# One order for all experts on three engines, outputs in two units of their own, and another depth of look-ahead

## The chip, the cores and the metric

The kernel runs on one core of one Trainium2 chip. The metric is the device time in microseconds (us) of one execution; three runs of the kernel before gave 1392.2, 1393.46 and 1393.85, so the median is 1393.46 us. Engines are named as in the profile: PE is TensorE (PEld its weight loads), DVE is VectorE, ACT is ScalarE, POOL is GpSimd, SP is SyncE, which here only issues transfers. A q after an engine's name is its sequencer.

## The reference

One decoder layer on 1024 tokens of width 1024. The first part (a gated MLP over chunks and differential attention, an output projection, cross-attention into 256 memory tokens) isn't touched by the change. The last part is a mixture of 32 experts with two experts for each token, and a norm:

```python
def hierarchical_moe(h, ...):            # t: 1024 tokens x 1024
    # group by softmax (top 1 of 4), then two of the 8 experts of that group, weights wts
    # tokens sorted by expert, in blocks of 128 rows, each block of one expert e
    def expert_rows(args):
        xb, e = args                      # xb: 128 x 1024
        g = xb @ w_gate[e]                # 1024 x 512
        u = xb @ w_up[e]                  # 1024 x 512
        return (jax.nn.silu(g) * u) @ w_down[e]   # 512 x 1024
    ...
    out = sum over the two experts of wts * y
x = x + hierarchical_moe(rms_norm(x, norm_ffn), ...)
return rms_norm(x, norm_final)
```

## The kernel before

All matmuls run in a form of float32 that is rounded, and each operand is split into a high part (a cast, on ACT) and a low part (the difference, on DVE). One product is then three matmuls (`mm3`, lines 135 to 138: high by high, high by low, low by high).

**An expert's work.** Expert e takes one block of up to 128 tokens. Its weights come as 12 tiles of 128 x 1024 (512 KB each): four of w_gate, four of w_up, four of w_down. Each tile is loaded by SP into a `raw` (line 271), split by ACT into `whi` (line 280) and by DVE into `wlo` (line 281), and used by six matmuls. `gather(e)` (line 1059) fetches the token rows by an indirect transfer of POOL into one of three `xg`. `x_t(e)` transposes them on PE (`px`, eight transposes, line 1414) and splits them into `xth` on ACT and `xtl` on DVE. `gate_up(e)` is 48 matmuls into two banks `pgu`, then Silu on ACT (`hh`, line 1436) and a product on DVE (`hh`, line 1437). `h_t(e)` turns `hh` (`pt`, four transposes, line 1444) and splits it into `ht`. `down(e)` is 24 matmuls into `py`, a copy `y` on ACT (line 1463) that applies the routing weight, and an indirect transfer of POOL that adds `y` to the rows of x2d in DRAM (line 1464), called the scatter here. A scatter waits until the one ahead of it has landed.

**The loop** (line 1489 on) does, for each e: `gate_up(e)`, `x_t(e + 1)`, `gather(e + 4)`, `down(e - 1)`, `h_t(e)`. After expert 1, `count_blocks` counts on PE and DVE how many blocks of 128 tokens are left over; at e = 4 that number is read into a register of each engine (line 1511), and a part behind the end, under `tc.If(nr > 0)`, handles leftover blocks. At e = 12 a row `gfin` for the last norm is loaded into a unit that stays taken.

**Memory.** `raw`, `whi`, `wlo`, `xth`, `xtl`, `ht`, `y`, `gfin` and the tiles of the end are *units*, 128 x 1024 words of float32 each, from one pool of NU = 45. A new tile takes a unit that is free in the program's order, and its writer waits for the last user of that unit. The planner `pump` issues loads up to `ahead["load"]` tiles ahead of the tile in use and splits up to `ahead["split"]` = 3 tiles ahead; each `take()` moves both on by one.

**Order.** SP and POOL always follow the order in which the program is written. PE, DVE and ACT follow it inside `tc.manual_schedule(engines=RM)`; outside, a scheduler places their instructions by a model of time. Before, the experts are outside from the end of expert 1 (`man.__exit__` at e = 1) to the start of the last pair (`last.__enter__` at e = 30). The look-ahead of the loads is `LF` = 10 from expert 16, ahead of that max(31, 30 - 2e) = 31.

Of the kernel before, what the change touches and what calls it, by code (L numbers as in the profile page):

```python
# [19 lines left out]
D = 1024  # L20
KT = 8
H = 512
NE = 32
NOV = 16
# [12 lines left out]
AL = 1  # L37
MD = 4.0
NX = 3
LA = 30  # L40
LE = 31
LD = 2
LS = 3
PF = 3
RM = {mybir.EngineType.DVE, mybir.EngineType.PE, mybir.EngineType.Activation}
PK = 12
LF = 10
EF = 16
JT = 0
ED = 1  # L50
KQ = lambda nc: nc.gpsimd
# [58 lines left out]
def tile_layer(tc, a, out):  # L110
    nc = tc.nc
# [11 lines left out]
    def unit(name, shape, dt=F32):  # L123
        return up.tile(shape, dt, name=name, tag="u", bufs=NU)
# [7 lines left out]
    def ps2(name="pd"):  # L132
        return psum.tile([128, 1024], F32, name=name, tag="pd", bufs=2)

    def mm3(o, sh, sl, mh, ml, start, stop):
        mm(o, sh, mh, start=start, stop=False)  # L136
        mm(o, sh, ml, start=False, stop=False)  # L137
        mm(o, sl, mh, start=False, stop=stop)  # L138
# [41 lines left out]
    def row(t, ap, n):  # L180
        nc.gpsimd.dma_start(t, bass.AP(tensor=ap.tensor, offset=ap.offset, ap=[[0, 128], [1, n]]))
# [81 lines left out]
    ahead = {"load": 3, "split": 1}  # L263
# [21 lines left out]
    def take():  # L285

        j = ptr["use"]
        ptr["use"] += 1
        pump()
        k = plan[j][1]  # L290
        return [t.rearrange("p (k c) -> p k c", k=k) for t in parts.pop(j)]
# [765 lines left out]
    def gather(e):  # L1057
        x = xg[e % NX]
        nc.gpsimd.indirect_dma_start(out=x, out_offset=None, in_=td[:, :],
                                     in_offset=bass.IndirectOffsetOnAxis(ap=idx[:, e:e + 1], axis=0),  # L1060
                                     bounds_check=S - 1, oob_is_err=False)
# [281 lines left out]
    man = tc.manual_schedule(engines=ORDS[0])  # L1343
# [39 lines left out]
    man = tc.manual_schedule(engines=ORDS[1])  # L1383
# [4 lines left out]
    man = tc.manual_schedule(engines=ORDS[2])  # L1388
# [6 lines left out]

    ahead["load"], ahead["split"] = LA, LS

    xts = {}
    def x_t(e):
        x = xg[e % NX]  # L1400
        if e == 0:
            xh, xl = unit("xth", [128, D], F32R), unit("xtl", [128, D], F32R)
            for i in range(2):
                p = ps1("px")
                cs = slice(512 * i, 512 * i + 512)
                for k in range(4):
                    nc.tensor.transpose(p[:, k * 128:(k + 1) * 128], x[:, (4 * i + k) * 128:(4 * i + k + 1) * 128],
                                        ident)
                split(xh[:, cs], xl[:, cs], p)
            xts[e] = (xh, xl)  # L1410
            return
        px = ps2("px")
        for k in range(KT):
            nc.tensor.transpose(px[:, k * 128:(k + 1) * 128], x[:, k * 128:(k + 1) * 128], ident)
        xh, xl = unit("xth", [128, D], F32R), unit("xtl", [128, D], F32R)
        split(xh, xl, px)
        xts[e] = (xh, xl)

    hts = {}

    def gate_up(e, between=None):
        xh, xl = xts.pop(e)
        gu = []
        for w in range(2):
            p = ps1("pgu")
            for q in range(4):
                wh, wl = take()
                for k2 in range(2):
                    k = 2 * q + k2
                    ks = slice(k * 128, (k + 1) * 128)  # L1430
                    mm3(p, xh[:, ks], xl[:, ks], wh[:, k2], wl[:, k2], k == 0, k == KT - 1)
            gu.append(p)
            if w == 0 and between:
                between()
        hh = half("hh")
        nc.scalar.activation(hh, gu[0], AF.Silu, scale=tab[:, 1, e:e + 1])
        nc.vector.scalar_tensor_tensor(hh, gu[1], tab[:, 1, e:e + 1], hh, op0=OP.mult, op1=OP.mult)
        hts[e] = hh

    def h_t(e):  # L1440
        hh = hts[e]
        pt = ps1("pt")
        for k in range(4):
            nc.tensor.transpose(pt[:, k * 128:(k + 1) * 128], hh[:, k * 128:(k + 1) * 128], ident)
        x = unit("ht", [128, 2, H], F32R)
        split(x[:, 0], x[:, 1], pt)
        hts[e] = x

    def down(e, between=None):
        x = hts.pop(e)  # L1450
        py = ps2("py")
        for k in range(4):
            wh, wl = take()
            ks = slice(k * 128, (k + 1) * 128)
            for c in range(2):
                cs = slice(c * 512, (c + 1) * 512)
                mm3(py[:, cs], x[:, 0, ks], x[:, 1, ks], wh[:, 0, cs], wl[:, 0, cs], k == 0, k == 3)
            if k == 1 and between:
                between()
        if e == NE - 1:  # L1460
            return py
        y = unit("y", [128, D])
        nc.scalar.activation(y, py, AF.Copy, scale=tab[:, 0, e:e + 1])  # L1463
        nc.gpsimd.indirect_dma_start(out=x2d[:, :], out_offset=bass.IndirectOffsetOnAxis(ap=idx[:, e:e + 1], axis=0),  # L1464
                                     in_=y, in_offset=None, bounds_check=S - 1, oob_is_err=False,
                                     compute_op=OP.add)

    man = tc.manual_schedule(engines=RM)
# [7 lines left out]
    novi = op.tile([128, 1], I32, name="novi")  # L1476

    def count_blocks():

        pc = ps1()  # L1480
        for t in range(8):
            mm(pc[:, :NE], oneb, Mb[t // 4][:, 3 + t % 4], start=(t == 0), stop=(t == 7))
        nc.vector.tensor_scalar(nb, pc[:, :NE], 128.0, None, op0=OP.is_gt)
        for j in range(2, 8):
            nc.vector.tensor_scalar(t1, pc[:, :NE], 128.0 * j, None, op0=OP.is_gt)
            nc.vector.tensor_add(nb, nb, t1)
        nc.vector.tensor_reduce(nov[:, 0:1], nb, axis=AX.X, op=OP.add)
        nc.vector.tensor_copy(novi, nov[:, 0:1])
    for e in range(NE):
        ahead["load"] = LF if e >= NE - EF else max(LE, LA - LD * e)  # L1490
        gate_up(e, between=(lambda: h_t(0)) if e == 1 else None)
        if e + 1 < NE:
            x_t(e + 1)
        if e + 1 + NX < NE:
            gather(e + 1 + NX)
        if e == NE - 2:
            last = tc.manual_schedule(engines=RM)
            last.__enter__()

            down(e - 1, between=lambda: h_t(NE - 2))  # L1500
            break
        if e:
            down(e - 1)
        if e:
            h_t(e)
        if e == 1:
            man.__exit__(None, None, None)
            count_blocks()
        if e == 4:
            with tc.manual_schedule(engines=RM):  # L1510
                nr = nc.values_load(novi[0:1, 0:1], min_val=0, max_val=NOV - 1,
                                    skip_runtime_bounds_check_because="2048 assignments leave at most 15 further blocks")
        if e == PK:
            gfin = unit("gfin", [128, D])
            row(gfin, a["norm_final"], D)


    e = NE - 1

    ahead["load"], ahead["split"] = 20, 5  # L1520
    down(e - 1)
    st = op.tile([128, 2, 9], F32, name="rfin")
    xf = [unit("xf", [128, D]) for _ in range(8)]
# [52 lines left out]
    for t in (0, 2, 3, 1, 4, 6, 5, 7):  # L1576
        store(t)
    nc.gpsimd.indirect_dma_start(out=out[:, :], out_offset=bass.IndirectOffsetOnAxis(ap=idx[:, NE - 1:NE], axis=0),  # L1578
                                 in_=sq[8], in_offset=None, bounds_check=S - 1, oob_is_err=False)
    last.__exit__(None, None, None)  # L1580

    ovu = {}
    ovp = [0]
# [15 lines left out]
    with tc.If(nr > 0):  # L1599
# [63 lines left out]
        with tc.For_i(0, nr, 1) as b:  # L1663
            eb = nc.values_load(eidd[bass.ds(b, 1), :], engines=[mybir.EngineType.SP], min_val=0, max_val=NE - 1,
                                skip_runtime_bounds_check_because="clamped to the last expert")
# [39 lines left out]
            y = unit("oy", [128, D])  # L1705
# [51 lines left out]
def _build(arrays):  # L1757
    import numpy as np
    import concourse.bacc as bacc
    nc = bacc.Bacc("TRN2", target_bir_lowering=False, num_devices=1)  # L1760
    a = {n[3:]: nc.dram_tensor(n, v.shape, mybir.dt.from_np(v.dtype), kind="ExternalInput").ap()
         for n, v in arrays.items()}
    out = nc.dram_tensor("out_0_dram", (S, D), mybir.dt.from_np(np.dtype("float32")), kind="ExternalOutput").ap()
    with tile.TileContext(nc, schedule_with_timeline_sim=True) as tc:
        tile_layer(tc, a, out)
    return nc
# [8 lines left out]
```

## Time and profile before

| | |
|---|---|
| median of three runs | 1393.46 us (1392.2 to 1393.85) |
| profiled execution | 1396.04 us, span of its instructions 1394.3 us |
| mean granted clock of TensorE | 0.974 |
| busy share of the span | PE 95%, PEld 82%, DVE 72%, ACT 60%, POOL 18% |
| moved by DMA | 322.39 MB, mean 231 GB/s |
| first matmul of an expert | 776.8 us |

The busy shares are means over the whole span. The experts fill the time from 776.8 us to about 1365 us, and there the engines are far busier than the means say; the part ahead of 776.8 us is the same program in both kernels.

### The profile page before, as it was taken

The page shows a single profiled execution, that of the slowest core. Times are in us where ns is not written, and L with a number is a line of the kernel's source. Part 1 is how long each engine was busy: PE and PEld are TensorE (multiplying, and loading weights), DVE is VectorE, ACT ScalarE, POOL GpSimd, SP SyncE. Part 2 cuts the span into 40 slices and gives each one's busy share as a digit, 9 for nine tenths or more (in the row PEclk, how much of TensorE's full clock was granted, in tenths as well). Part 3 has the DMA queues.
Part 4 walks back from the last instruction along what each step waited for, and adds up shares of the span by engine and source line. Part 5 has one row for each costly group of instructions (what it writes and reads, how often), then busy time and mean ns, then how long its engine had stood idle before and what let it go on. Part 6 is the DMA issues. An engine that isn't in the chain of part 4 may idle for free. (4 is left out here: it accounts for less than half of the span.)

```text
span 1394.3 us, 20530 instructions
## 1 busy us (share of the span) xinstructions
PE 1322.7 (95%) x7424; PEld 1146.8 (82%) x7424; DVE 1001.3 (72%) x1564; ACT 836.7 (60%) x1139; POOL 255.7 (18%) x284
## 2 busy tenths in 40 slices
PE   7999999999989999999998899999989999999981
PEld 6988998989888889998886687888778888888861
DVE  6776694767765543434365798999979999999984
ACT  6644553445455543333323587888868888888874
POOL 2521110411021321112112121111111111111110
PEclk9999999999999999999998799999999999999995
DMA  8720211320275664103799799999999699999986
GB/s 306 220 84 15 47 61 46 91 69 16 101 266 188 201 243 143 38 25 110 241 331 336 244 322 369 364 355 357 354 366 351 226 371 381 366 366 363 373 287 256
DMA packets 103226, 322.39 MB, mean 231 GB/s; under 512 B 15748, under 2 KB 23972, under 8 KB 103121
## 3 DMA queue, kind: packets, MB, share of 16 engines
q1 hardware_dynamic: 76896, 272.14, 53.4%
q0 software_dynamic: 17776, 40.51, 10.1%
q10 hardware_dynamic: 8448, 8.39, 1.8%
q8 instruction: 59, 0.97, 0.3%
q14 instruction: 47, 0.38, 0.1%
HBM read 287.10 MB, written 46.66 MB: 239 GB/s over the span
## 5 line engine op out<-in xcount | busy, mean ns | idle before, releaser
L281 DVE TENSOR_TENSOR wlo<-raw,whi 128x1024 fp32r<-128x1024 f32 (+1 forms) x469 | 559.6, 1231 | 75.3 <-ACT whi L280 62.6
L280 ACT CAST whi<-raw 128x1024 fp32r<-128x1024 f32 (+1 forms) x469 | 472.7, 1050 | 69.2 <-DVE wlo L281 11.9
L136 PE MATMUL pgu<-whi,xth 128*128 128x512 f32 x512 | 199.4, 398 | 4.3 <-ACT whi L280 3.2
L137 PE MATMUL pgu<-wlo,xth 128*128 128x512 f32 x512 | 201.2, 393 | 0.8 <-DVE wlo L281 0.8
L138 PE MATMUL pgu<-whi,xtl 128*128 128x512 f32 x512 | 201.0, 393 | 0.5 <-DVE xtl L142 0.5
L1464 POOL DMA_INDIRECT x2d<-y,idx x31 | 51.6, 1666 | 449.4 <-ACT y L1463 411.5
L136 PEld LDWEIGHTS pgu<-whi,xth 128*128 128x128 f32 x512 | 97.0, 190 | 26.0 <-ACT whi L280 5.2
L137 PEld LDWEIGHTS pgu<-wlo,xth 128*128 128x128 f32 x512 | 97.2, 190 | 22.3 <-DVE wlo L281 1.4
L138 PEld LDWEIGHTS pgu<-whi,xtl 128*128 128x128 f32 x512 | 97.0, 189 | 21.2 <-DVE xtl L142 1.2
L137 PE MATMUL py<-wlo,ht 128*128 128x512 f32 x256 | 103.7, 405 | 2.2 <-DVE wlo L281 2.2
L136 PE MATMUL py<-whi,ht 128*128 128x512 f32 x256 | 102.3, 399 | 1.5 <-ACT whi L280 0.8
L138 PE MATMUL py<-whi,ht 128*128 128x512 f32 x256 | 101.0, 394 | 0.0
L658 ACT ACTIVATE p<-p,stt 128x128 f32<-128x128 f32 (+7 forms) x64 | 49.6, 776 | 50.4 <-DVE stt L657 45.9
L136 PE MATMUL pp<-whi,hTh 128*128 128x256 f32 x256 | 74.6, 291 | 0.2 <-ACT whi L280 0.2
L137 PE MATMUL pp<-wlo,hTh 128*128 128x256 f32 x256 | 73.4, 287 | 1.3 <-DVE wlo L281 1.3
L136 PE MATMUL pp<-whi,h2h 128*128 128x256 f32 x256 | 73.1, 285 | 0.0
L138 PE MATMUL pp<-whi,hTl 128*128 128x256 f32 x256 | 73.1, 285 | 0.0
L137 PE MATMUL pp<-wlo,h2h 128*128 128x256 f32 x256 | 72.5, 283 | 0.0
L138 PE MATMUL pp<-whi,h2l 128*128 128x256 f32 x256 | 72.5, 283 | 0.0
L136 PE MATMUL pp<-hTh,whi 128*128 128x512 f32 x160 | 63.6, 397 | 0.4 <-ACT ot L710 0.4
L137 PE MATMUL pp<-hTl,whi 128*128 128x512 f32 x160 | 63.0, 394 | 0.0
L138 PE MATMUL pp<-hTh,wlo 128*128 128x512 f32 x160 | 62.8, 393 | 0.0
(365 smaller groups left out, 2942.4 us busy)
## 6 DMA issues: line engine op xcount, KB each, us to landing
raw<-in_w_gate SPq DMA_DIRECT2D x128, 512.0 KB
raw<-in_w_up SPq DMA_DIRECT2D x128, 512.0 KB
raw<-in_w_down SPq DMA_DIRECT2D x128, 512.0 KB
raw<-in_w_in SPq DMA_DIRECT2D x19, 512.0 KB
raw<-in_w_kv_mem SPq DMA_DIRECT2D x16, 512.0 KB
raw<-vwd SPq DMA_DIRECT2D x16, 512.0 KB
raw<-in_w_q_memT SPq DMA_DIRECT2D x8, 512.0 KB
raw<-in_w_out SPq DMA_DIRECT2D x8, 512.0 KB
```

Of the source, the lines that this page charges most:

```text
L136: mm(o, sh, mh, start=start, stop=False)
L137: mm(o, sh, ml, start=False, stop=False)
L138: mm(o, sl, mh, start=False, stop=stop)
L280: nc.scalar.copy(hi[:, c], raw[:, c])
L281: ahead.get("lo", nc.vector).tensor_tensor(lo[:, c], raw[:, c], hi[:, c].bitcast(F32), op=OP.subtract)
L658: nc.scalar.activation(pe[:, :nk], pe[:, :nk], AF.Exp, bias=stt[:, 2 + m:3 + m], scale=slopes[hd], accum_out=stt[:, 4 + m:5 + m])
L1464: nc.gpsimd.indirect_dma_start(out=x2d[:, :], out_offset=bass.IndirectOffsetOnAxis(ap=idx[:, e:e + 1], axis=0), in_=y, in_offset=None, bou ...
```

## The change

The experts are now one manual stretch on PE, DVE and ACT from expert 0 to the end of the kernel, so the three engines follow the order of the loop. The two tiles `ys` are taken once, ahead of the loop, and `y` of expert e is `ys[e % 2]`; the other tiles share 43 units. `ahead["load"]` is 29 up to expert 11 (e < PK = 12) and 27 from expert 12 on.

```diff
-LA = 30
-LE = 31
-LD = 2
+LA = 29
+LE = 29
 PK = 12
-LF = 10
-EF = 16
...
     hts = {}
+    ys = [unit("y", [128, D]) for _ in range(2)]
...
         if e == NE - 1:
             return py
-        y = unit("y", [128, D])
+
+        y = ys[e % 2]
         nc.scalar.activation(y, py, AF.Copy, scale=tab[:, 0, e:e + 1])
...
     for e in range(NE):
-        ahead["load"] = LF if e >= NE - EF else max(LE, LA - LD * e)
+        ahead["load"] = LE if e < PK else LE - 2
         gate_up(e, between=(lambda: h_t(0)) if e == 1 else None)
...
         if e == NE - 2:
-            last = tc.manual_schedule(engines=RM)
-            last.__enter__()
 
             down(e - 1, between=lambda: h_t(NE - 2))
             break
...
         if e == 1:
-            man.__exit__(None, None, None)
             count_blocks()
         if e == 4:
-            with tc.manual_schedule(engines=RM):
-                nr = nc.values_load(novi[0:1, 0:1], min_val=0, max_val=NOV - 1,
+            nr = nc.values_load(novi[0:1, 0:1], min_val=0, max_val=NOV - 1,
...
-    last.__exit__(None, None, None)
+    man.__exit__(None, None, None)
```

Line numbers of the changed kernel are two to five lower for the same statement.

**ACT in the steady part of the experts** (expert 20 and its neighbours). Before, one expert reads:

```order
L1463 ACTIVATE y<-py,tab 128x1024
L141 CAST ht<-pt 128x512
L280 CAST whi<-raw 128x1024 x4
L1436 ACTIVATE hh<-pgu,tab 128x512
L280 CAST whi<-raw 128x1024 x4
L141 CAST xth<-px 128x1024
L280 CAST whi<-raw 128x1024 x4
```

In the changed kernel the same stretch reads:

```order
L1462 ACTIVATE y<-py,tab 128x1024
L138 CAST ht<-pt 128x512
L277 CAST whi<-raw 128x1024 x8
L1434 ACTIVATE hh<-pgu,tab 128x512
L138 CAST xth<-px 128x1024
L277 CAST whi<-raw 128x1024 x4
```

The Silu moves four splits later, directly ahead of the split of the next expert's tokens. On PE the loop's order now holds word for word: all 48 matmuls of `gate_up(e)`, the eight transposes of `x_t(e + 1)`, the 24 matmuls of `down(e - 1)`, the four transposes of `h_t(e)`; before, both kinds of transposes stood between matmuls of `down`.

**ACT at the second tile of w_up of expert 13** (`whi_10020` before, `whi_9998` now), with the semaphores that each row waits for; DMAHW is a load by SP, DMASW an indirect transfer of POOL. Before:

```order
L280 CAST whi_9996<-raw_9572 128x1024 [waits DMAHW1_49,DVE_49]
L280 CAST whi_10008<-raw_9584 128x1024 [waits DMAHW2_49,PE_49]
L280 CAST whi_10020<-raw_9596 128x1024 [waits DMAHW3_49,DMASW0_49]
L280 CAST whi_10032<-raw_9608 128x1024 [waits DMAHW4_49,DMASW2_49,Activation_49]
L1436 ACTIVATE hh_10091<-pgu_9993,tab_96 128x512 [waits PE_49]
```

Now:

```order
L1462 ACTIVATE y_7662<-py_9908,tab_96 128x1024 [waits DMASW6_49,PE_49]
L138 CAST ht_9966<-pt_9961 128x512 [waits PE_49]
L277 CAST whi_9974<-raw_9581 128x1024 [waits DMAHW1_49]
L277 CAST whi_9986<-raw_9593 128x1024 [waits DMAHW2_49,DVE_49,PE_49]
L277 CAST whi_9998<-raw_9618 128x1024 [waits DMAHW3_49,DVE_49,PE_49]
L277 CAST whi_10010<-raw_9630 128x1024 [waits DMAHW4_49,DVE_49,PE_49]
```

Before, the unit of `whi_10020` was that of an earlier `y`, and the split waits until that `y`'s scatter has landed. Now no split up to expert 30 waits for a scatter; `y` itself waits for the scatter of two experts earlier.

**DVE after expert 1**, at `count_blocks` (`nb`, `t1`, `nov`: counts of 128 x 32). Before, from the split of the turned hidden tile on:

```order
L142 TENSOR_TENSOR ht_7984<-pt_7979,ht_7984 128x512
L1485 TENSOR_SCALAR t1_7686<-ps_7988 128x32
L1486 TENSOR_TENSOR nb_7685<-nb_7685,t1_7686 128x32
L281 TENSOR_TENSOR wlo_8016<-raw_7414,whi_8015 128x1024
L1485 TENSOR_SCALAR t1_7686<-ps_7988 128x32
L281 TENSOR_TENSOR wlo_8028<-raw_7416,whi_8027 128x1024
```

Now the whole count follows that split, and this is its end and what comes next:

```order
L1484 TENSOR_SCALAR t1_7688<-ps_7984 128x32
L1485 TENSOR_TENSOR nb_7687<-nb_7687,t1_7688 128x32
L1486 TENSOR_REDUCE nov_7689<-nb_7687 128x1
L1487 CAST novi_7690<-nov_7689 128x1
L278 TENSOR_TENSOR wlo_8012<-raw_7414,whi_8011 128x1024
```

The 15 small instructions of the count stood among the splits of expert 2; now all of them stand in one piece ahead of the next split. The read of the register stood in the last part of the program on PE, DVE and ACT, and now stands there at expert 5.

## Rows read from the trace of the kernel before

**Rows 1.** The page: busy us, share and instructions of each engine.

```profile
PE 1322.7 (95%) x7424; PEld 1146.8 (82%) x7424; DVE 1001.3 (72%) x1564; ACT 836.7 (60%) x1139; POOL 255.7 (18%) x284
```

**Rows 2.** Timeline of ACT: the Silu of experts 2, 4, 10, 12, 13, 16, 29.

```profile
818.69 0.69 ACT L1436 ACTIVATE hh<-pgu,tab 128x512 f32<-128x512 f32 x1 [0.33 <-PE pgu L138]
...
856.69 0.68 ACT L1436 ACTIVATE hh<-pgu,tab 128x512 f32<-128x512 f32 x1
...
963.07 0.68 ACT L1436 ACTIVATE hh<-pgu,tab 128x512 f32<-128x512 f32 x1
...
999.85 0.69 ACT L1436 ACTIVATE hh<-pgu,tab 128x512 f32<-128x512 f32 x1
...
1022.66 0.68 ACT L1436 ACTIVATE hh<-pgu,tab 128x512 f32<-128x512 f32 x1
...
1077.37 0.69 ACT L1436 ACTIVATE hh<-pgu,tab 128x512 f32<-128x512 f32 x1
...
1307.39 0.69 ACT L1436 ACTIVATE hh<-pgu,tab 128x512 f32<-128x512 f32 x1 [0.28 <-PE pgu L138]
```

**Rows 3.** Timeline of ACT: two splits, with the idle time ahead of them.

```profile
842.63 1.99 ACT L280 CAST whi<-raw 128x1024 fp32r<-128x1024 f32 x2 [3.23 <-DMA x2d<-y,idx]
...
1021.71 1.04 ACT L280 CAST whi<-raw 128x1024 fp32r<-128x1024 f32 x1 [4.30 <-issue]
```

**Rows 4.** Timeline of POOL: issues of four scatters.

```profile
832.31 1.59 POOL L1464 DMA_INDIRECT x2d<-y,idx  x1 [15.35 <-ACT y L1463]
...
1012.87 1.58 POOL L1464 DMA_INDIRECT x2d<-y,idx  x1 [14.58 <-DVE wlo L281]
...
1338.99 2.49 POOL L1464 DMA_INDIRECT x2d<-y,idx  x1 [16.48 <-ACT y L1463]
1350.42 2.41 POOL L1464 DMA_INDIRECT x2d<-y,idx  x1 [8.93 <-ACT whi L280]
```

**Rows 5.** Windows of 18 us: busy by engine, PEclk, DMA share, GB/s.

```profile
1005.00:1023.00 18.00, 15.03 (x70) 11.52 (x68) 12.33 (x13) 10.98 (x13) 3.30 (x3) 1.00 0.97 349
...
1077.00:1095.00 18.00, 18.00 (x87) 15.01 (x86) 16.60 (x16) 14.87 (x17) 3.02 (x2) 1.00 0.33 87
...
1329.00:1347.00 18.00, 17.22 (x76) 13.46 (x75) 16.30 (x16) 15.73 (x17) 2.49 (x1) 1.00 1.02 383
```

**Rows 6.** Waits of SP from 1060 to 1110 us: total, times, longest.

```profile
SPq L271 <- DVE wlo L281: 20.6, 4, 17.5
```

**Rows 7.** Timelines of PE and DVE in expert 1.

```profile
804.79 1.03 PE L1414 MATMUL px<-ident,xg 128*128 128x128 f32 x8
...
809.79 0.39 PE L136 MATMUL py<-whi,ht 128*128 128x512 f32 x1
...
806.91 1.23 DVE L142 TENSOR_TENSOR xtl<-px,xth 128x1024 fp32r<-128x1024 f32 x1 [0.31 <-ACT xth L141]
808.05 4.62 DVE L281 TENSOR_TENSOR wlo<-raw,whi 128x1024 fp32r<-128x1024 f32 x4
```

**Rows 8.** Timeline of DVE: the first and the fifth instruction of the count.

```profile
812.87 0.19 DVE L1483 TENSOR_SCALAR nb<-ps 128x32 f32<-128x32 f32 x1 [0.20 <-PE ps L1482]
...
813.65 0.22 DVE L1486 TENSOR_TENSOR nb<-nb,t 128x32 f32<-128x32 f32 x1
```

**Rows 9.** The tile novi: the register's read on PE's sequencer, ns and start.

```profile
L1511 PEldq TENSOR_LOAD <-novi x1: 491/491/491, 1361.1 to 1361.1; - x1
```

**Rows 10.** Waits of ACT from 1270 to 1360 us: total, times, longest.

```profile
ACT whi L280 <- DMA raw<-in_w_down: 8.8, 10, 1.8
```

**Rows 11.** Timelines of ACT, PE, SP at the end: outputs of experts 29, 30.

```profile
1337.59 1.12 ACT L1463 ACTIVATE y<-py,tab 128x1024 f32<-128x1024 f32 x1
...
1345.04 1.11 ACT L1463 ACTIVATE y<-py,tab 128x1024 f32<-128x1024 f32 x1
...
1357.17 0.66 PE L1444 MATMUL pt<-ident,hh 128*128 128x128 f32 x4 [2.90 <-DVE hh L1437]
...
1357.85 4.52 SPq L1526 DMA_DIRECT2D xf<-x2d  x8
```

More of the change, by code (lines that the diff above doesn't have):

```diff
@@ L1506, in tile_layer @@
         if e == 1:
-            man.__exit__(None, None, None)
             count_blocks()
         if e == 4:
-            with tc.manual_schedule(engines=RM):
-                nr = nc.values_load(novi[0:1, 0:1], min_val=0, max_val=NOV - 1,
-                                    skip_runtime_bounds_check_because="2048 assignments leave at most 15 further blocks")
+            nr = nc.values_load(novi[0:1, 0:1], min_val=0, max_val=NOV - 1,
+                                skip_runtime_bounds_check_because="2048 assignments leave at most 15 further blocks")
         if e == PK:
```

## The prediction

> **What bounds it now.** The page's busy shares [rows 1] put PE far ahead, but they are means over stages, so I read stage by stage. From 776.8 us on the experts run, and the Silu on ACT marks each expert once. From expert 16 to expert 29 it comes 13 times in 1307.39 - 1077.37 = 230.02 us, 17.69 us apart [rows 2], and the window there shows PE busy for all of its 18.00 us [rows 5]: in this stretch PE is the bound, and no order on the other engines can make it shorter. Elsewhere experts take longer. From 2 to 29 there are 488.70 us for 27 steps, where 27 x 17.69 = 477.63 would do: 11.07 us are lost. They sit in two places [rows 2]: 2 to 4 takes 38.00 us (2.62 too many), 10 to 16 takes 114.30 us (8.16 too many, of which 22.81 - 17.69 = 5.12 in the one step from 12 to 13); 4 to 10 loses 0.24, 16 to 29 loses 0.05.
>
> Next, why. In both bad steps one split on ACT stands idle for long: 3.23 us at 842.63, put down to the landing of a scatter, and 4.30 us at 1021.71 [rows 3]. The second has no releaser in the view, but the order of the kernel before shows that split waiting for an indirect transfer of POOL, and a scatter was issued at 1012.87 [rows 4], 8.84 us ahead; the first was issued at 832.31, 10.32 us ahead. A scatter lands about 9 to 10 us after its issue, and the unit of its `y` was given to a split.
>
> What is left of the second place (8.16 - 5.12 = 3.04 us) I put down to a shortage of units. With 31 raws, two `y`, four token tiles and one `ht` out of 45, about 7 units are left for whi and wlo, three and a half pairs, where the look-ahead of 3 wants four; `gfin` takes one more at expert 12. This cause is argued from a count, not read.
>
> Last the transfers. DMA is full nearly everywhere (share 0.97 and 1.02 in the first and last window of [rows 5]), except from 1077 to 1095 us, where it is 0.33: SP stands 17.5 us in one wait [rows 6], because the look-ahead falls from 31 to 10 at expert 16 and a load far ahead of its use has to wait for a unit. That loses 0.67 x 18 = 12.1 us of transfers, and nobody misses them until the end, where ACT waits ten times for loads, 8.8 us in all [rows 10]. So the loads are a second bound just behind PE.
>
> **The change, part by part.**
>
> *Stalls removed.* With `ys` apart, no split up to expert 30 waits for a scatter. The other tiles share 43 units: 43 - 29 raws - 4 - 1 leaves 9, from expert 12 on 43 - 27 - 1 - 4 - 1 = 10, more than four pairs. So both causes go, and I take all of it: -11.1 us. Bounds: at least the two steps with a landing (5.12 and most of 2.62, say -7), at most -11.1, since PE fills the rest. The new wait is that `y` waits for the scatter of two experts earlier; behind it on ACT stand `ht` and eight splits, and PE waits for these. It was issued 2 x 17.69 us earlier and lands within 10.3 us, so the cover is some 25 us; gone, it would cost the landing's 10 us per expert. A split near the end takes the unit of expert 29's output; its landing (by 1350.42 in the old trace, [rows 4]) comes ahead of PE's need for the last hidden tile.
>
> *The fixed order itself.* The trace holds a sample of it: expert 1 ran under the loop's order. PE starts the transposes at 804.79; DVE splits the tokens at 806.91 and then four weight tiles from 808.05, 4.62 us for four, so the first, which is the fourth tile of `down`, is done by 809.2; PE comes to that tile at 809.79 [rows 7]. The order keeps up with 0.6 us to spare, at the tightest place. Cost taken 0; bounds 0, and the rival below.
>
> On SP and POOL nothing changes place but the register's read, two rows earlier on SP, so every load, gather and scatter keeps its rank in its queue; only the units that they wait for differ.
>
> *The count on DVE in one piece.* Its first five instructions start 0.78 us apart over four steps [rows 8], 0.195 each, so 15 take 2.9 us, now ahead of the next split. DVE is busy 16.60 of 18 us [rows 5], so 1.4 us per expert can absorb it: +1.5 us once. Bounds 0 and 2.9.
>
> *The register.* It was read where PE had nothing urgent, 491 ns [rows 9]; now it stands between two experts on PE, DVE and ACT. On PE it can lie behind queued transposes (0) or in front of the matmuls (0.5). I take +0.5.
>
> *Look-ahead.* Starting with 29 instead of 31 makes the loads two tiles later where they are ahead, 2 x 17.69 / 12 = 2.9 us. The change from 29 to 27 at expert 12 holds back two loads for a moment, where 31 to 10 held back 21, so the 12.1 us come back. The stream of loads thus ends 12.1 - 2.9 = 9.2 us earlier. PE comes to the last experts 11.1 - 1.5 - 0.5 = 9.1 us earlier. The loads just follow: no gain and no loss at this point, but no slack either.
>
> *The end.* From `y` of expert 29 at 1337.59 to the first load of the sum at 1357.85 [rows 11] there are 20.26 us, made of two scatters in a row, 11.43 us from 1338.99 to 1350.42 and 7.43 us to 1357.85 [rows 4, 11]. `y` of expert 30 at 1345.04 is there in time and doesn't count; nor does PE's 2.90 us wait for the last `hh`, since what follows hangs on the loads of the sum. If the waits for loads shrink, `y` of expert 29 is up to 2.9 us less late (0 to 2.9, I take 1.0). The two scatters are 7.4 to 11.4 us each: -4.0 to +4.0 against now, taken 0 because transfers still run then. So -1.0 here.
>
> **The sum.** -11.1 + 1.5 + 0.5 - 1.0 = -10.1 us. The profiled execution took 1396.04 us (its span is 1394.3, with 1.7 around it), so it would take 1385.9. It is 2.6 us over the median of the runs, 1393.46, and the median goes to 1383.4 us, 0.7% less.
>
> One rule speaks against this. The window in which splits can run ahead gets narrower in the second half: with a look-ahead of 10 some 27 units were free for pairs, now 10. The rows say that this is enough, since experts 4 to 10 ran with about 7 and took 106.38 us for six, 17.73 each [rows 2]; by them the sum stays 1383.4. The Trainium skill (Perfetto Trace Analysis, Identifying Performance Opportunities) says that the same gap repeating on the engine that should be saturated can mean too little SBUF for the next tile; it gives no figure, and by it the third rival would hold, 1397.4.
>
> **Rivals.**
>
> *The loads are late* (0.18). The 9.2 us against 9.1 leave nothing, and the end already waits for loads [rows 10]. For it: DMA is full in every window but one. Against: the first half had loads long ahead. Every us that the stream lacks costs one; if it comes only half as early, 4.6 us are missing: 1388.0.
>
> *The end shortens* (0.12). If the loads are drained when expert 29's scatter goes, both scatters take the shorter time: -4.0 more, 1379.4.
>
> *A gap in every expert* (0.10), the other side. The 0.6 us at the fourth tile of `down` [rows 7] is thin, and expert 1 had loads and units in plenty. Should ACT come to a split late, the same gap returns 28 times. It decides from 10.1 / 28 = 0.36 us a time; at 0.5 us it costs 14: 1397.4.
>
> *The stalls stay* (0.08). If experts 10 to 16 lose their time to full transfers (0.97 at 1005 us, [rows 5]) and not to units, only the first place goes: -2.6 - 1.0 + 2.0 = -1.6, 1391.9.
>
> **Numbers.** The forecast has 0.52, and its own range is 1379 to 1387. With the late loads (0.18), and most of the short end (0.10 of 0.12), 0.80 lie from 1377.5 to 1391. About 0.2% (2.8 us) can be told from no change here. Faster: 0.52 + 0.12 + 0.16 of the late loads = 0.80. Same: the stalls that stay and the rest of the late loads, 0.10. Slower: 0.10.
>
> **What would show it.** In the changed profile the Silus should lie 17.7 us apart from expert 4 to 29, with some 2 us lost once near expert 2; no split waits for a landing; DMA has no window under 0.9 between 830 and 1320 us. Repeated idle time of PE with ACT or DVE as releaser would be the gap; waits of ACT for loads from expert 24 on would be the late loads. The prediction is wrong if DMA, once never idle, moves less in a time than it did, or if the fixed order makes PE wait at places that expert 1 does not show.

## The result, and the profile after

The changed kernel takes 1385.55 us (median; 1383.87 to 1386.86), the kernel before 1393.65 in the runs beside it (1392.2 to 1394.88). The ratio is 0.9938, 95% interval 0.9924 to 0.9952: 8.1 us faster, where 10.1 were forecast. A second measurement on another chip gave 1386.01 against 1392.36, ratio 0.9953 (0.9937 to 0.9969), 6.4 us. The profiled execution of the changed kernel took 1386.86 us, its span is 1385.2; that of the kernel before was 1396.04 and 1394.3, so in the traces 9.1 us are gone.

The page's busy row, which answers to [rows 1]: the counts of instructions are the same. PE's busy time falls by 4.6 us; part of that is stretches at the lower granted clock that the trace of before has and this one has not, shown under "The order alone" and "The sum".

```profile
PE 1318.1 (95%) x7424; PEld 1145.2 (83%) x7424; DVE 1001.0 (72%) x1564; ACT 842.3 (61%) x1139; POOL 245.7 (18%) x284
```

The Silus of [rows 2] are no good marks across the change, since their place among the splits on ACT has moved. The issue of an expert's scatter on POOL is one: it follows PE's last matmul of `down`. Timeline of POOL in the changed kernel, scatters of experts 1, 11, 14, 24, 28, 29 and 30 (start, us, line, what, and in brackets the idle time ahead of it):

```profile
831.68 1.59 POOL L1463 DMA_INDIRECT x2d<-y,idx  x1 [5.59 <-ACT y L1462]
...
1009.00 1.58 POOL L1463 DMA_INDIRECT x2d<-y,idx  x1 [5.61 <-ACT y L1462]
...
1062.39 1.58 POOL L1463 DMA_INDIRECT x2d<-y,idx  x1 [5.78 <-ACT y L1462]
...
1239.53 1.59 POOL L1463 DMA_INDIRECT x2d<-y,idx  x1 [5.60 <-ACT y L1462]
...
1313.04 1.80 POOL L1463 DMA_INDIRECT x2d<-y,idx  x1 [15.78 <-ACT y L1462]
1331.26 1.78 POOL L1463 DMA_INDIRECT x2d<-y,idx  x1 [16.43 <-ACT y L1462]
1341.87 1.56 POOL L1463 DMA_INDIRECT x2d<-y,idx  x1 [8.82 <-DMA x2d<-y,idx]
```

The same view of the kernel before for experts 14, 24 and 28; experts 1, 11, 29 and 30 stand in [rows 4].

```profile
1073.51 1.58 POOL L1464 DMA_INDIRECT x2d<-y,idx  x1 [14.45 <-ACT y L1463]
...
1249.97 1.59 POOL L1464 DMA_INDIRECT x2d<-y,idx  x1 [14.37 <-ACT y L1463]
...
1320.81 1.71 POOL L1464 DMA_INDIRECT x2d<-y,idx  x1 [15.76 <-ACT y L1463]
```

After less before: -0.6 us at expert 1, -3.9 at 11, -11.1 at 14, -10.4 at 24, then -7.8 at 28, -7.7 at 29, -8.5 at 30. So the two bad places are gone, and some 2.7 us are given back between experts 24 and 28. Windows of the changed kernel (busy by engine, PEclk, DMA share, GB/s):

```profile
1005.00:1023.00 18.00, 18.00 (x87) 14.96 (x86) 16.83 (x16) 15.15 (x18) 3.29 (x3) 1.00 0.98 368
1077.00:1095.00 18.00, 18.00 (x87) 14.96 (x86) 16.73 (x16) 15.39 (x17) 2.62 (x2) 1.00 0.98 356
1257.00:1275.00 18.00, 17.21 (x82) 13.96 (x82) 15.46 (x15) 14.15 (x17) 3.39 (x2) 1.00 1.03 378
1275.00:1293.00 18.00, 16.84 (x79) 13.64 (x78) 15.17 (x15) 14.26 (x16) 1.97 (x1) 1.00 0.97 358
1329.00:1347.00 18.00, 17.15 (x76) 13.88 (x74) 16.37 (x15) 15.18 (x16) 3.34 (x2) 1.00 0.83 272
```

Against [rows 5]: from 1005 us PE is now busy for all 18.00 us instead of 15.03, and the hole of the loads at 1077 (0.33) has closed (0.98). New are the two windows from 1257 us, where PE loses 0.79 and 1.16. Timeline of ACT there, the Silu of five experts and one split:

```profile
1231.15 0.67 ACT L1434 ACTIVATE hh<-pgu,tab 128x512 f32<-128x512 f32 x1
1249.99 0.68 ACT L1434 ACTIVATE hh<-pgu,tab 128x512 f32<-128x512 f32 x1
...
1266.69 1.05 ACT L277 CAST whi<-raw 128x1024 fp32r<-128x1024 f32 x1 [2.46 <-DMA raw<-in_w_down]
...
1268.91 0.68 ACT L1434 ACTIVATE hh<-pgu,tab 128x512 f32<-128x512 f32 x1
...
1288.06 0.68 ACT L1434 ACTIVATE hh<-pgu,tab 128x512 f32<-128x512 f32 x1
...
1305.71 0.68 ACT L1434 ACTIVATE hh<-pgu,tab 128x512 f32<-128x512 f32 x1
```

The steps are 18.84, 18.92 and 19.15 us, then 17.65, and a split stands 2.46 us for a load: the late loads of the first rival. The waits of ACT from 1250 to 1335 us (total, times, longest) say the same; [rows 10] is the like row of before, with no loss on PE up to 1329 us.

```profile
ACT whi L277 <- DMA raw<-in_w_down: 9.3, 7, 2.5
```

### The profile page after: what moved, and what is told of

It reads as the page before. It is cut to its first block, busy times and chain, and to the rows that moved or that the text cites. A ratio compares the mean times of both kernels' runs of the same rounds, so it can differ in the third digit from the quotient of the medians.

```text
span 1385.2 us, 20568 instructions
## 1 busy us (share of the span) xinstructions
PE 1318.1 (95%) x7424; PEld 1145.2 (83%) x7424; DVE 1001.0 (72%) x1564; ACT 842.3 (61%) x1139; POOL 245.7 (18%) x284
## 5 line engine op out<-in xcount | busy, mean ns | idle before, releaser
L133 PE MATMUL pgu<-whi,xth 128*128 128x512 f32 x512 | 203.4, 397 | 1.1 <-ACT xth L138 1.1
L134 PE MATMUL py<-wlo,ht 128*128 128x512 f32 x256 | 100.9, 394 | 1.9 <-DVE wlo L278 1.9
L1056 POOL DMA_INDIRECT xg<-td,idx x32 | 35.3, 1102 | 296.1 <-PE px L1411 273.9
```

## The experiments

The theory: units that come back from a scatter, and too few units, made the two stalls; with them gone the stream of loads is the bound of the last experts and takes some of the gain back. The rivals: the fixed order makes the gain; or the fixed order, with its narrower window for splits, makes the loss at experts 24 to 28. All ratios are to the kernel before on the same chip.

| run | median us | ratio (95%) |
|---|---|---|
| y_shared | 1389.09 | 0.9970 (0.9960 to 0.9980) |
| sched_order | 1407.55 | 1.0101 (1.0080 to 1.0121) |
| look_old | 1389.75 | 0.9982 (0.9971 to 0.9994) |
| order_only | 1396.75 | 1.0039 (1.0016 to 1.0061) |
| half_down2 | 1383.19 | 0.9942 (0.9925 to 0.9958) |
| after_again | 1386.01 | 0.9953 (0.9937 to 0.9969) |
| count_spread | 1387.32 | 0.9957 (0.9941 to 0.9973) |
| lead31 | 1386.43 | 0.9945 (0.9928 to 0.9961) |
| lead33 | 1390.79 | 0.9978 (0.9964 to 0.9991) |
| lead33_count | 1385.65 | 0.9946 (0.9931 to 0.9962) |
| lead31_long | 1386.14 | 0.9955 (0.9939 to 0.9972) |

### The units undone

```diff
-        y = ys[e % 2]
+        y = unit("y", [128, D])
```

> The changed kernel, but each expert's output takes a unit of the common pool again (order and look-ahead stay). My theory (units handed from a scatter to a split, and a full stream of loads behind it): splits wait for a scatter's landing again, one of them for 2 us or more near expert 13, and the time goes up from 1385.55 by 2 to 6 us, to 1387.5 to 1391.5; less than the 8 us that the two bad places cost before, since the loads, which are late at experts 25 to 28 by 2.7 us, use the time that PE loses. Rival (the fixed order made the gain, the units did nothing): 1385.5 within 1.5, no split waits for a landing for over 1 us.

As the theory had it: 1389.09. Timelines of DVE and ACT in y_shared, near expert 13:

```profile
1021.04 4.71 DVE L278 TENSOR_TENSOR wlo<-raw,whi 128x1024 fp32r<-128x1024 f32 x4 [3.34 <-issue]
```

```profile
1022.30 2.19 ACT L277 CAST whi<-raw 128x1024 fp32r<-128x1024 f32 x2 [4.52 <-DVE wlo L278]
```

DVE stands 3.34 us until 1021.04; the scatter of expert 11, issued at 1011.90, lands at 1021.0, and ACT's next split waits behind it. DVE stands so twice more, 2.07 us until 821.27 and 2.92 until 843.01; the view names ACT there, but the scatters of experts 0 and 1 land at 821.19 and 842.93, and all three splits start 0.08 us behind a landing. Against the changed kernel the scatters are 2.9 us later from expert 2 to 11, 4.9 later from expert 12 to 25 and 4.1 later at expert 30: the late loads hide a part, as expected. The stall near expert 13 alone is worth 1.9 us here.

### The order undone

```diff
         if e == 1:
+            man.__exit__(None, None, None)
             count_blocks()
...
         if e == NE - 2:
+            last = tc.manual_schedule(engines=RM)
+            last.__enter__()
```

> The changed kernel, but experts 2 to 29 are put in order by the scheduler again (units of their own and look-ahead stay). My theory: the order is worth nothing by itself; the count on VectorE is spread again, so experts 2 to 24 run 1 to 1.5 us earlier, and the loads take that back at experts 25 to 28: 1385.5 within 2. The scatter of expert 24 is issued 11 to 13 us earlier than in the kernel before, that of expert 28 again only 8 to 9. Rival (the fixed order made the gain): 1390 to 1394, with the stalls near experts 2 to 4 and 10 to 16 back. Second rival (the fixed order, with its narrow window for splits, makes the loss at experts 25 to 28): the steps there are 17.7 us, and the time is 1382 to 1383.

All three expectations failed: 1407.55, 22 us over the changed kernel and 14 over the kernel before. Waits of PE in sched_order (total, times, longest):

```profile
PE py L133 <- DVE xtl L139: 16.5, 11, 2.4
PE pt L1442 <- DVE hh L1435: 7.9, 8, 1.7
```

Neither has its like in the changed kernel, where PE waits for `hh` once, 2.0 us at the end. The scheduler, given outputs in units of their own and 29 tiles of look-ahead, puts out another order than in the kernel before, and in it, by the releasers named, PE waits again and again for `hh` and for the split of the next tokens. Why it chooses that order was not looked into, and what each wait costs is not shown.

### The look-ahead undone

```diff
-        ahead["load"] = LE if e < PK else LE - 2
+        ahead["load"] = LF if e >= NE - EF else max(LE, LA - LD * e)
```

with `LA, LE, LD, LF, EF` as before.

> The changed kernel, but with the old look-ahead: 31 tiles, 10 from expert 16 (order and units stay). My theory: the stream of loads pauses for about 12 us at expert 16 and starts 2.9 us further ahead; it is already the bound at the end, so all of the difference shows: 1385.55 + 12.1 - 2.9 = 1394.8, 1391 to 1396, with waits of ScalarE for loads from about expert 22 on. Experts 12 to 15, with 2 units less for splits, take 0.3 to 1 us more each. Rival (loads don't bound the end; the loss at experts 25 to 28 has another cause): the shortage in experts 12 to 15 alone, 1387 to 1389.

1389.75, over the rival's range and under the theory's: about 4 to 6 us slower than the changed kernel by the two ratios of that one, not 9.2. Timeline of POOL in look_old, scatters of experts 11 and 15:

```profile
1007.70 1.58 POOL L1466 DMA_INDIRECT x2d<-y,idx  x1 [5.53 <-ACT y L1465]
...
1081.67 1.59 POOL L1466 DMA_INDIRECT x2d<-y,idx  x1 [5.61 <-ACT y L1465]
```

These four experts take 73.97 us; in the changed kernel 1079.93 - 1009.00 = 70.93. No split waits for a scatter here, so 3.04 us is the price of the two to four units that are missing. Then the loads pause, 15.5 us in one wait of SP. Ahead of it they were issued 6 us earlier than in the changed kernel (expert 17's w_up from 1047 and 1053 us): 2.9 from the two tiles more, the rest since this execution began its experts earlier (the scatter of expert 0 is issued 3.4 us earlier). Behind it, at expert 20, they are 5.5 us later (1115.7 and 1110.2). So the pause cost the stream 11.8 us, close to my 12.1. What I missed comes after it: the loads of the next four experts take 70.9 us instead of 75.1, so 4.2 us are regained. At expert 24 the loads are 1.3 us later (1186.6 and 1185.3), and the scatter of expert 30 is 1.6 later (1343.43). This run alone doesn't tell whether loads or units set its end: counted from the scatter of expert 0, PE is 5.2 us behind the changed kernel at expert 15 already, and 5.0 at expert 30.

### The order alone

The kernel before with the fixed order and nothing else.

> The kernel before with the fixed order alone: outputs in units of the common pool, look-ahead 31 and 10 from expert 16. My theory: the order alone brings nothing, since splits still get the units of scatters and are short of units: stalls of several us near experts 12 and 13 as in the kernel before, 1391 to 1395. Rival (the fixed order makes the gain by itself, and the run sched_order showed the price of leaving it): 1385 to 1388.

1396.75 (1388.56 to 1404.37), 0.4% slower than the kernel before: the rival that the order alone makes the gain is out. The executions differ widely: five of twelve took 1400 us or more, with a mean granted clock of 0.972 to 0.974, against 0.979 in the one of 1388.56; only one of 1394.49 has a trace. Timelines of ACT and of POOL in order_only (a split ahead of expert 13; scatters of experts 11 and 15):

```profile
1017.53 3.88 ACT L280 CAST whi<-raw 128x1024 fp32r<-128x1024 f32 x4 [4.74 <-issue]
```

```profile
1008.49 1.58 POOL L1465 DMA_INDIRECT x2d<-y,idx  x1 [6.66 <-DVE wlo L281]
...
1087.62 1.59 POOL L1465 DMA_INDIRECT x2d<-y,idx  x1 [5.61 <-ACT y L1464]
```

The wait for a landing is back (4.74 us, [rows 3] had 4.30), and the four experts take 79.13 us. With order and look-ahead fixed, the three kernels split the second bad place: 79.13 - 73.97 = 5.16 us for the units that come from scatters, 73.97 - 70.93 = 3.04 for the shortage.

The 5.16 are not all waiting. Windows of order_only, then of the kernel before, at the stall and behind it (busy by engine, PEclk, DMA share, GB/s):

```profile
1015.00:1020.00 5.00, 1.56 (x7) 0.74 (x5) 1.30 (x2) 2.47 (x3) 0.00 (x0) 0.91 0.96 372
1020.00:1025.00 5.00, 5.00 (x13) 3.88 (x14) 3.98 (x4) 3.05 (x4) 0.00 (x0) 0.50 1.00 379
1030.00:1035.00 5.00, 5.00 (x26) 4.12 (x25) 4.41 (x5) 4.60 (x6) 1.61 (x1) 1.00 1.03 410
```

```profile
1020.00:1024.00 4.00, 1.19 (x5) 0.41 (x3) 1.21 (x1) 2.29 (x3) 0.00 (x0) 1.00 1.02 403
1024.00:1028.00 4.00, 3.93 (x10) 3.11 (x11) 3.58 (x4) 3.32 (x4) 0.00 (x0) 0.57 0.94 363
```

Behind the stall TensorE's granted clock falls to its lower level (0.50, 1.2 instead of 2.4 GHz): in order_only for 6.8 us, in which PE does 13 matmuls in 5 us where it does 26 at 1.00, so some 3.4 of the 5.16 us are lost there. In the kernel before the lower level lasts 3.4 us (0.57 over 4 us) and costs some 1.7; there the four experts take 78.15 us. In y_shared the clock stays at 1.00 at this place, and the units cost 1084.78 - 1011.90 - 70.93 = 1.95 us. So what units from scatters cost depends on how long PE stands and on the clock behind it.

### Less to load

The edit, cut, as it stands in half_down2; in half_down `hl` is `k == 1`.

```diff
+            hl = k == 1 and j >= nx0
-            for i in ((0, 512), (512, 1024)) if j == 0 else ((0, 1024),):
+            for i in ((0, 512), (512, 1024)) if j == 0 else ((0, 512 if hl else 1024),):
...
+                    rb = raw[:, None, 0:512].to_broadcast([128, 2, 512])
```

> The changed kernel with half of each tile of w_down loaded (512 columns, which the split on ScalarE and VectorE reads twice, so that every engine's work stays; the output is another one): DMA carries one twelfth of 2 MB less per expert, 5 tiles for 6. My theory: the loads keep their lead, the steps at experts 25 to 28 are 17.7 us again (-2.7), and the last two scatters, with DMA less full, take 7 to 9 us each (-1 to -4): 1385.55 - 2.7 - 2.5 = 1380.4, 1378.5 to 1382.5. Rival (the narrow window for splits makes the loss): the steps at 25 to 28 stay at 18.8 to 19.1 us, 1384 to 1386.

In half_down the cut also caught tiles of the same shape in the stages ahead, so other tokens went to the experts, and the blocks for experts with over 128 tokens ran behind the last expert: its 1469.28 us can't be set beside the others. Its experts can: they are 17.7 us apart up to expert 28. half_down2 cuts the experts' tiles alone.

> As the run half_down, but only the experts' w_down tiles are halved, so that everything ahead of the experts, the routing too, is that of the changed kernel (the output of the experts is another one). In the run before, the experts' steps stayed at 17.73 us to the end and the sum's loads could start 6.3 us earlier, counted from the scatter of expert 24. My theory (late loads): the same here, 1385.55 - 2.7 at experts 25 to 28 - 3.6 at the last scatters = 1379.3, 1377.5 to 1381.5. Rival (the loss at experts 25 to 28 is the window for splits): 1384 to 1386.

Timeline of POOL in half_down2, scatters of experts 24, 28, 29, 30:

```profile
1235.53 1.59 POOL L1471 DMA_INDIRECT x2d<-y,idx  x1 [5.60 <-ACT y L1470]
...
1306.46 1.56 POOL L1471 DMA_INDIRECT x2d<-y,idx  x1 [16.15 <-ACT y L1470]
1324.68 1.56 POOL L1471 DMA_INDIRECT x2d<-y,idx  x1 [16.66 <-ACT y L1470]
1331.46 2.25 POOL L1471 DMA_INDIRECT x2d<-y,idx  x1 [5.22 <-ACT y L1470]
```

From 24 to 28 it is 70.93 us, 17.73 an expert; in the changed kernel 73.51. The engines' work and the window for splits are the same (from 1100 to 1200 us DVE is busy for 92.97 us, in the changed kernel for 93.06), the bytes are a sixth fewer, and in half_down it is 70.93 us too: in these traces the loss at experts 24 to 28 is the loads', and the rival of the narrow window is out. The scatter of expert 30 now waits last for its own `y` and not for the landing of 29's (6.78 us after it instead of 10.61).

The times say less than the trace. The traced execution took 1375.70 us, under the 1377.5 expected, and it is the shortest of six; of its 11.2 us under the changed kernel's, 4.0 are an earlier first expert (772.72 against 776.68 us). The median, 1383.19, lies between the two expected ranges, and its ratio isn't clear of after_again's. The executions go with their mean granted clock. At 0.979 half_down2 took 1375.70 and after_again 1381.75; at 0.977 it took 1380.1 to 1383.38, the changed kernel 1385.72 and 1385.93; at 0.975 it took 1385.62, the changed kernel 1386.86 and 1388.8. So fewer bytes are worth some 1 to 6 us, and the size stays open.

### Where the gain in PE's time goes

after_again is the changed kernel once more; count_spread deals out the count, one of its instructions on DVE in each call of `take` (cut: the rest of the edit puts the 15 instructions into `pend`):

```diff
+        if pend:
+            pend.pop(0)()
```

> The changed kernel itself, as a measure beside the next three on the same chip: 1385.5 within 1.5.

> The changed kernel with the 15 instructions of the count on VectorE dealt out, one ahead of each of the next 15 tiles, instead of in one piece. My theory: the scatters of experts 2 to 24 are issued 1 to 1.5 us earlier, and the late loads take it back by expert 28, so the time stays at 1385.5 within 1. Rival (PE is the bound to the end): 1384.2, with the scatter of expert 30 as much earlier as that of expert 11.

Timeline of POOL in after_again, scatters of experts 24, 28, 30:

```profile
1237.28 1.91 POOL L1463 DMA_INDIRECT x2d<-y,idx  x1 [4.97 <-ACT y L1462]
...
1312.74 1.81 POOL L1463 DMA_INDIRECT x2d<-y,idx  x1 [15.75 <-ACT y L1462]
...
1341.88 1.56 POOL L1463 DMA_INDIRECT x2d<-y,idx  x1 [9.12 <-DMA x2d<-y,idx]
```

This execution is 2.25 us ahead of the first at expert 24 and level with it at 30 (1341.88, 1341.87): PE's lead is gone into waits for loads. count_spread shows it again: expert 11 is 1.8 us earlier (1007.2), expert 30 is 1.2 later (1343.09). The time, 1387.32, is above the 1386.5 that were expected at most; beside after_again's 1386.01 it is no gain, and the rival's 1384.2 is out.

### More lead for the loads

```diff
-        ahead["load"] = LE if e < PK else LE - 2
+        ahead["load"] = 31 if e < 2 else LE if e < PK else LE - 2
+        ahead["load"] = 31 if e < 10 else 29 if e < 14 else 27
```

The first new line is lead31 (33 in lead33 and lead33_count, the latter with the count dealt out), the second lead31_long; ahead of the experts the look-ahead is 31 or 33 too.

> The changed kernel with a look-ahead of 31 tiles ahead of the experts and in experts 0 and 1, 29 from expert 2 on. My theory (the stream of loads, full from 810 us on, sets the time of the last experts): two tiles more of lead stay until the end, 2 x 17.7 / 12 = 2.9 us; the loss at experts 25 to 28 goes nearly whole, and the scatter of expert 30 is issued at 1339 to 1340 in place of 1341.9: 1386 - 2.5 = 1383.5, 1382 to 1385. Rival (the last experts hang on something other than the lead of the loads): 1385.5 to 1387.

> As lead31, with 33 tiles ahead of the experts and in experts 0 and 1. My theory: 4 tiles of lead, 5.9 us, of which only the 2.7 lost at experts 25 to 28 and some of the end can be had; splits are short of units in experts 0 and 1 (0.2 to 1 us each): 1381 to 1384. Rival: the shortage of units at the start costs more than that, or the lead is worth nothing: 1386 to 1389.

> lead33 with the count on VectorE dealt out over 15 tiles, as in count_spread, where it moved nothing because the loads were late. My theory: with more lead the loads are late by less, so that part of the 1.2 us comes through: 1380 to 1383.5, some 0.5 us under lead33. Rival: as lead33.

> The changed kernel with a look-ahead of 31 tiles until expert 9, 29 in experts 10 to 13, 27 after. In lead31 the two tiles of lead were given back at expert 2, where DMA fell to 0.94 between 810 and 830 us; here they are kept until the loads are 8 in flight at all times. My theory (the loads set the time of the last experts): the slack of the loads at expert 16 is 2 to 3 us more, the scatter of expert 30 is issued 1.5 to 3 us earlier than in the changed kernel (1341.9 in both of its traces), 1383 to 1384.5; experts 3 to 9 take 17.9 us in place of 17.73, as in look_old, for want of units, and that costs nothing at the end. Rival (lead is worth nothing at the end): 1386 to 1388, the scatter of expert 30 at 1342 or later.

No lead came through in the medians: 1386.43, 1390.79, 1385.65, 1386.14. My theory's numbers failed in all four; the rivals of lead31 and lead31_long came true, those of the other two didn't. In lead31 the lead is given back as soon as the look-ahead falls: from 810 to 830 us DMA moves 304 GB/s (share 0.94), in after_again 362 (1.00). In lead31_long it is kept, but 31 raws leave two units less for splits: experts 4 to 8 take 17.9 us, the scatter of expert 8 comes 1.9 us later than in the changed kernel (957.7, 955.8), and later loads wait for PE's units. The slack at expert 16 is some 3 us more, as expected; yet 1.9 of it are PE's delay, the loads themselves are issued 1.6 us earlier there (1031.8 and 1033.4 us), and at expert 24 they are level (1184.9 and 1185.3). lead33 loses 1.6 us more between experts 0 and 1 (scatters 21.5 us apart, 19.9 in the changed kernel); its granted clock is 0.91 from 810 to 830 us, where the changed kernel has 1.00. lead33_count, which is lead33 with the count dealt out, has 1.00 there and 17.4 us, and its median is 5.1 us lower. So at this look-ahead the count in one piece costs more than the 1.5 us that it costs in the changed kernel; by which path was not tried. No version beats the changed kernel by more than its interval.

That the lead runs brought nothing doesn't speak against the loads, since hardly any lead was left at the end. Only in the trace of lead33_count are the last loads earlier than in the changed kernel (expert 31's first w_up by 2.1 us, 1322.77), and there the scatter of expert 30 is 2.2 earlier (1339.72); that execution began its experts 2.0 us earlier, and its median is no better. One distance binds them: from the first w_up load of expert 31 to the scatter of expert 30 there are 16.9 to 17.3 us in the changed kernel (1324.90 and 1341.87), in after_again, y_shared, look_old, count_spread and all four lead runs, though their scatters of expert 24 lie up to 9 us apart (1235.24 in lead33_count, 1244.41 in y_shared). From 1250 to 1329 us SP waits 58 of 79 us for earlier loads in the changed kernel, so there the loads wait for one another and hardly for PE. In half_down2 the distance is 38.2 us, and SP waits for no load.

## Why the prediction held, point by point

**What bounds it.** PE first, and the loads "a second bound just behind PE": right, but the second was read from the DMA share and so not sized. Timeline of SP in the changed kernel, the w_up loads of experts 12 and 24:

```profile
955.30 4.63 SPq L268 DMA_DIRECT2D raw<-in_w_up  x4
...
1185.32 4.93 SPq L268 DMA_DIRECT2D raw<-in_w_up  x4
```

That is (1185.32 - 955.30) / 12 = 19.2 us per expert, where PE needs 17.7: the loads live off their lead and lose 1.5 us of it with each expert. Whom SP waits for tells which it is, here from 950 to 1250 us in the changed kernel, then in half_down2:

```profile
SPq L268 <- DMA raw<-in_w_down: 77.7, 62, 3.2
SPq L268 <- DMA raw<-in_w_gate: 69.7, 57, 3.1
SPq L268 <- DMA raw<-in_w_up: 67.9, 59, 3.3
SPq L268 <- DVE wlo L278: 5.6, 17, 0.9
```

```profile
SPq L270 <- PE pgu L135: 76.9, 48, 2.6
SPq L270 <- DVE wlo L286: 65.6, 71, 2.5
```

In the first a load waits for earlier loads to land, in the second for PE and DVE to give a unit back.

**Stalls removed**, -11.1 with the register's +0.5: from expert 1 to 14 the trace gained 10.5 (-0.6 to -11.1), forecast 10.6. The two causes, of which the shortage was only argued, measured 5.16 and 3.04 us in the second place; the prediction had 5.12 and 3.04. That the first agrees is luck: the 5.12 of the kernel before hold some 1.7 us at the lower granted clock, the 5.16 of order_only some 3.4, and the prediction took both for waiting alone. With the shorter look-ahead (y_shared) the same cause costs 1.95 there.

**The fixed order**, 0: nearly. Experts 14 to 24 take 17.71 us each instead of 17.65, +0.7 over the ten. From 15 to 24 it is 17.73 in the changed kernel, order_only and look_old, and 17.66 in the kernel before. But the sample of expert 1 said only that the order keeps up, not what else the scheduler would have done: sched_order shows that without it the two other parts cost 14 us.

**The count**, +1.5: PE loses 1.57 us in one wait for a split ahead of 817.03 us, behind the 15 instructions from 812.65 to 815.82 us (timeline of PE):

```profile
817.03 0.50 PE L134 MATMUL pgu<-wlo,xth 128*128 128x512 f32 x1 [1.57 <-DVE wlo L278]
```

**The register**, +0.5: nothing; it is read on PE's sequencer at 863.8 us in 485 ns, and PE is busy for all of 830 to 900 us. That was the lower bound.

**Look-ahead**, "no gain, no loss, no slack": this is the step that failed in size. Loads came about as much earlier as worked out (the first of expert 29's w_up at 1282.0 us against 1290.5, 8.5 for 9.2). PE came 10.4 earlier at expert 24 and only 7.7 at expert 29, so 2.7 were lost: +2.7 where the prediction had 0. The rival of the late loads gave 1388.0 by half of the 9.2; it was the right mechanism with a smaller price, and its sign, waits of ACT for loads from expert 24 on, came. What was missed is the pace: a stream slower than PE at 19.2 to 17.7 gives back whatever PE gains, late and at the end. That the 8.5 us come so near to the 9.2 is luck, since its terms missed by some 3 us each: at expert 17 the loads of the changed kernel are 0.2 us behind those of the kernel before and not 2.9 (1053.4 and 1053.2), the pause cost 14.8 us by expert 20 and not 12.1 (1110.2 and 1124.8), and 6.2 of that, which the prediction didn't have, were regained by expert 28 (1263.2 and 1271.6).

**The end**, -1.0: -1.3 by the rows. The two scatters in a row took 10.61 and 6.93 us (from 1331.26 to 1341.87 and to the sum's loads at 1348.80), against 11.43 and 7.43 [rows 4, 11]. SP's row of the changed kernel:

```profile
1348.80 4.16 SPq L1521 DMA_DIRECT2D xf<-x2d  x8
```

**The sum.** In the traces -0.6 up to expert 1, -10.5 to expert 14, +0.7 to 24, +2.7 to 29 and -1.3 at the end are -9.0, of the 9.1 measured. The -0.6 are -1.8 at the scatter of expert 0 and +1.2 for the count. No term of the prediction had the -1.8, and most of that belongs to the two executions. Windows of the kernel before and of the changed one:

```profile
792.00:796.00 4.00, 3.87 (x10) 3.08 (x11) 2.44 (x3) 1.76 (x2) 0.00 (x0) 0.57 0.74 229
792.00:796.00 4.00, 3.48 (x16) 2.66 (x15) 4.00 (x4) 3.26 (x4) 0.00 (x0) 1.00 0.89 318
```

The granted clock falls in the first and not in the second; in order_only, which loads and splits by the rules of the kernel before up to there, it stays at 1.00, and in count_spread, which up to there is the changed kernel, it falls to 0.63. From the first matmul to that scatter the two traces of the changed kernel differ too, 35.1 and 33.8 us. So some 7 us of the 9.1 are left for the change; the medians gave 8.1 and 6.4.

Of the other rivals the stalls that stay did not come; the short end needs loads that are done earlier, which only the half_down runs had. The gap in every expert did not come with 29 raws. With 31 and the fixed order each of experts 4 to 8 takes 17.9 us (look_old and lead31_long) instead of 17.73, while the kernel before, with 31 under the scheduler's order, takes 17.69. The Trainium skill (Perfetto Trace Analysis, Identifying Performance Opportunities) says that the same gap repeating on the engine that should be saturated can mean too little SBUF for the next tile. The longer step repeats here, but a gap is not seen: look_old's PE is busy for all of 882 to 954 us, with 340 matmuls against 343 in the changed kernel.

## What to carry to other kernels

When a stall of the main engine is removed, compare the pace of the next stream, in us per round and not by its share, with that engine's: a slower stream that lives off its lead takes the gain back at the end, far from the edit. Buffers that a slow transfer hands back should not feed the tight pool, and buffers spent on depth of look-ahead are missing elsewhere: here two to four units were worth 3 us in four rounds. Look at the granted clock behind a stall before you price it: here it made 3.4 of 5.16 us. Try the parts of a change together as well as alone: here the order alone lost, two parts without it lost more, and all three gained.

## What the runs showed of the hardware

**A busy share near 1 is not a full DMA.** From 1100 to 1200 us half_down2 has a share of 0.95 at 325 GB/s, and neither ACT nor SP waits for a load there; the changed kernel has 0.99 at 357 GB/s, and its loads fall behind by 1.5 us per expert.

**A stall can cost more than its length.** In order_only PE is busy for 1.56 of the 5 us from 1015 us on, and behind that the granted clock is 0.50 for 6.8 us; in y_shared PE is busy for 8.38 of the 10 us from 1020 us on, and the clock stays at 1.00.

**A load is as late as its slowest parts.** The landing of a load is counted in 16 steps in the trace. From those (medians over the 12 tiles of an expert, us after the issue):

```
                        issued    8th    13th   last
changed,    expert 4      808     5.3     5.8    6.6
changed,    expert 16    1033     5.0    10.0   12.6
changed,    expert 24    1185     5.3     9.9   13.0
look_old,   expert 18    1066     5.6     6.1    6.8   (just ahead of and behind its pause)
look_old,   expert 24    1187     5.5    11.4   13.0
half_down2, expert 24    1163     4.2     5.5    6.4
```

In these rows half of the parts are there within 6 us of the issue. Where loads fall behind, the last ones come up to 7 us later: the last four in the changed kernel (the twelfth part is there at 5.7 and 6.1 us at experts 16 and 24), one or two more in look_old at expert 24. In the changed kernel from 950 to 1250 us 95% of the loads are issued within 0.1 us (median 0.06) after the load eight ahead has landed whole. So the stream goes at the pace of a few of the 16. A third of half_down2's loads are half as long. The Trainium skill (DMA: Bandwidth & Descriptors, Why a DMA increments its semaphore by 16 and not by 1) says that the 16 engines of a transfer finish independently and that only the full count means that the data is there; the trace agrees with the first (5.0 us for the eighth part and 12.6 for the last, at expert 16), and no run here shows the second. Which four they are isn't in the trace, and whether the gathers and scatters make them slow was not tried.
